# The fourth product of C and B in an accumulator bank, and the low inputs last in the first group of the mixer's output product

## The chip, the core and the metric

The kernel runs on one core of a Trainium2 chip. The metric is device time in microseconds (us) of one execution of the whole program. The core has a tensor engine (TensorE; PE for its matmuls and PEld for its weight loads in the profile), a vector engine (VectorE, DVE), an activation engine (ScalarE, ACT), a general engine (GpSimd, POOL) and a queue engine that issues transfers (SyncE, SP). Matmuls write into PSUM, which this kernel uses as eight banks of 128 x 512 floats.

## What is computed

The reference is a decoder trunk of two layers over 256 tokens of width 1024. Each layer has a SwiGLU feed-forward half step, a mixer, and a second feed-forward half step. The mixer is cut here to the parts that the change touches.

```python
def ssd_chunked(x, dt, a, Bm, Cm):                      # Mamba-2, chunks of 128 tokens
    ...
    cb = jnp.einsum("bclgn,bcsgn->bclsg", Cc, Bc)       # 4 groups g, 2 chunks c
    y_diag = jnp.einsum("bclsg,bclsgh,bcsghp->bclghp", cb, decay, xdt)
    ...
for l in range(DEPTH):
    h = h + 0.5 * swiglu(rms_norm(h, ffn1_norm[l]), ffn1_w_in[l], ffn1_w_out[l])
    u = rms_norm(h, mix_norm[l])
    (z_s, xbc, dt_s, qkv, z_d, b_d, a_d, gate_s, gate_d) = jnp.split(u @ w_in[l], split_points, axis=-1)
    y_s = mamba2_branch(z_s, xbc, dt_s, ...)
    y_d = deltanet_branch(qkv, z_d, b_d, a_d, ...)
    merged = (jax.nn.sigmoid(gate_s) * (y_s @ ssm_w_branch[l])
              + jax.nn.sigmoid(gate_d) * (y_d @ dn_w_branch[l]))
    h = h + merged @ w_out[l]
    h = h + 0.5 * swiglu(rms_norm(h, ffn2_norm[l]), ffn2_w_in[l], ffn2_w_out[l])
return rms_norm(h, final_norm)
```

## The kernel before

**Split products.** Every large product is made from a high and a low half of each factor: `hi` is the value rounded to a shorter format, `lo` what the rounding left. `mm3` (line 334) issues three matmuls for each block: high input times high weight (line 335), high input times low weight (line 336), low input times high weight (line 337). Below they are called A, B and C. `mm3w` and `tok_chunk` (lines 339 to 374) do the same with the roles of weight and input turned.

**Weights.** They stream from memory as tiles of 128 x 1024, issued by SyncE at line 171 into five buffers (`wraw`). `prep` (line 174) makes `whi` on ScalarE (the helper of line 68) and `wlo` on VectorE (the helper of line 71), each in five buffers. `take` (line 202) hands the next weight tile to the product that uses it and prepares up to five ahead.

**Order.** The kernel is written as one sequence. A planner puts it in order for each engine when the program is built, by the sequence, by priorities (work inside `tc.high_priority` comes 400 places earlier) and by its own estimate of when each instruction's inputs and buffers are ready. On the chip each engine then runs its list in that order and waits where an input is not ready. In the mixer the sequence follows a list of names, `ORDER` (line 46): the last part that matters here reads `x01 R d3 R R P R g100 g101 D0 S0 x10 T0 D1 x11 g110 g111 S1 x20 T1`. `R` advances the DeltaNet recurrence (`recur`), `P` is `ssd_pre`, `g` a gate product (`tok_chunk`, tile `t`), `D` the decay matrices (`decay`, tile `dc`, on VectorE and ScalarE), `x` a convolved product (tile `xs`, then three VectorE steps `ca` and a ScalarE step into `xsT`), `S` the head of one Mamba group (`ssd`: eight transposes `xsb` of `xsT`, then VectorE products), `T` its tail.

**PSUM.** Eight banks lie in two pools of four: `accb` (tag "acc") for accumulated products, `trb` (tag "tr") for transposes and short products. A tile of a pool can be written when an earlier tile's last reader is done.

**The product of C and B.** `ssd_pre` makes it for four groups (line 1043). For each group two matmuls (lines 1045 and 1046) write a bank `cbb`, VectorE masks two of its blocks into `cbm`, and ScalarE copies the third into `cbx` (both are parts of the tile `cbt`). All four banks come from the "tr" pool. Just ahead of it in the sequence the recurrence's last chunk takes "tr" banks too; the last of them is `ob` (line 993), which VectorE reads in `vb <- ob, os` (line 998). After that line 1002 to line 1008 square it, reduce it (`so`), take a power on GpSimd, and multiply `vb` by the result.

**The mixer's output product.** The merged branches pass through `merge(t)` (line 1256) for token tile t = 0, then 1: for each half n of the width VectorE makes `mt` and `tg`, TensorE transposes it (`mT`, line 1264), ScalarE makes the high input `mh` and VectorE the low input `ml`. Both calls run at high priority. Then `close` (line 437) issues `out_chunks` for the eight blocks k of the inner width: k = 0 and 1 as one group, k = 2 alone, and k = 3 to 7 as one group. A group goes through token tile 0 and then token tile 1. For tile 0 the order is n = 0 with all k, then n = 1 with all k, and each (k, n) issues A, B and C. The inputs of k = 0 to 3 all come from the transposed half n = 0 of `merge`. Each output bank `o` is an "acc" bank: `po[t][n]`. `close` is called nowhere else.

Of the kernel before, what the change touches and what calls it, by code (L numbers as in the profile page):

```python
# [24 lines left out]
GS = 4  # L25
# [28 lines left out]
def trunk_kernel(ctx, tc, x, wst, wsm, norms, lpar, rpar, cst, out):  # L54
    nc = tc.nc
    V, A, G, PE = nc.vector, nc.scalar, nc.gpsimd, nc.tensor
# [10 lines left out]
    def act(o, i, func=AF.Copy, **kw):  # L67
        return A.activation(out=o, in_=i, func=func, **kw)  # L68

    def tt(o, a, b, op):  # L70
        return V.tensor_tensor(out=o, in0=a, in1=b, op=op)  # L71
# [15 lines left out]
    def trb(name):  # L87
        return trp.tile([P, 512], F32, tag="tr", name=name)

    def accb(name):  # L90
        return accp.tile([P, 512], F32, tag="acc", name=name)
# [57 lines left out]
    state = {"loaded": 0, "prepped": 0, "taken": 0, "last": None, "hold": False, "behind": {}, "late": {}, "first": 0, "turns": {}, "first_chunk": False, "cap": n_forms}  # L149
# [52 lines left out]
    def take():  # L202
        j = state["taken"]
        state["taken"] = j + 1
        ahead("loaded", limit[min(j + NSPL, n_forms) - 1], load)
        ahead("prepped", min(j + 1 if state["hold"] else j + NSPL, n_forms, state["cap"]), prep)
        return halves.pop(j)
# [126 lines left out]
    def mm3(ps, lh, ll, rh, rl, start, stop):  # L334
        PE.matmul(ps, lh, rh, start=start, stop=False)  # L335
        PE.matmul(ps, lh, rl, start=False, stop=False)  # L336
        return PE.matmul(ps, ll, rh, start=False, stop=stop)  # L337
# [55 lines left out]
                        cut and a == 0 and kt == 1,  # L393
                    )

    def out_chunks(ps, stat, ks, last, group=1, split=False, first=None):

        for g0 in range(0, len(ks), group):
            kk = ks[g0 : g0 + group]
            ws = [(k, take()) for k in kk]  # L400
            for t in range(2):
                order = [(k, n) for n in range(2) for k in range(len(kk))]
                if t == 1 and not split:
                    m = len(kk) - 2 if len(kk) == NSPL else len(kk)
                    order = [(k, n) for k in range(m) for n in range(2)]
                    order += [(k, n) for n in range(2) for k in range(m, len(kk))]
                order = [(k, n, 0, 512) for k, n in order]
                if t == 1 and split:
                    order = [o for o in order if o[1] == 0]
                    order += [(k, 1, c, c + 256) for c in (0, 256) for k in range(len(kk))]  # L410
                state["sums"] = []
                for k, n, c0, c1 in order:
                    k, (wh, wl) = ws[k]
                    sh, sl = stat(k, t)
                    c = slice(n * 512 + c0, n * 512 + c1)
                    begin = k == 0 if first is None else first and t == n == 1
                    bank = ps[t][n][:, c0:c1]
                    if c0:
                        begin, bank = k == kk[0], ps[2][:, 0:256]
                    ins = mm3(bank, sh, sl, wh[:, c], wl[:, c], begin, k == last)  # L420
                    state["sums"].append(ins)

    def residual(po, nw):
        def add(t):
            banks = [(po[t][n][:], n * 512) for n in range(2)]
            if nw is None and t == 1:
                banks.append((po[2][:, 0:256], 768))
            for bank, c0 in banks:
                hv = h[:, t, c0 : c0 + bank.shape[-1]]
                ins = stt(hv, bank, 0.5, hv, ALU.mult, ALU.add)  # L430
            return ins

        if nw is None:
            return add
        norm_in(nw, add)

    def close(po, stat, n_k, nw):

        out_chunks(po, stat, list(range(2)), n_k - 1, group=2)
        out_chunks(po, stat, list(range(2, n_k - NSPL)), n_k - 1)  # L440
        state["hold"] = True
        out_chunks(po, stat, list(range(n_k - NSPL, n_k)), n_k - 1, group=NSPL, split=nw is None)
        return residual(po, nw)
# [149 lines left out]
    def mixer(l, nxt):  # L593
# [444 lines left out]
        def ssd_pre():  # L1038
            BT, CT = late["BC"][:, 0:4], late["BC"][:, 4:8]
            cbt = slots.tile([P, 3 * GS, P], F32, tag="sF", name="cbt")  # L1040
            late["cbx"] = cbx = cbt[:, 2 * GS :]
            late["cbm"] = cbm = cbt[:, : 2 * GS].rearrange("p (g t) l -> p g t l", g=GS)
            for g in range(GS):
                cbb = trb("cbb")
                PE.matmul(cbb[:, 0 : 2 * P], BT[:, g, 0:P], CT[:, g, :], start=True, stop=True)
                PE.matmul(cbb[:, 2 * P : 3 * P], BT[:, g, P : 2 * P], CT[:, g, P : 2 * P], start=True, stop=True)
                tt(
                    cbm[:, g],
                    cbb[:].rearrange("p (t o l) -> p t o l", t=2, o=2)[:, :, 0, :],
                    U[:, None, :].to_broadcast([P, 2, P]),  # L1050
                    ALU.mult,
                )
                act(cbx[:, g], cbb[:, P : 2 * P])
            yield
# [123 lines left out]
        def branch(kind, n, mk, tail=1):  # L1178
            ps = [[accb("b"), accb("b")] for _ in range(2)]
            held = {}  # L1180

            def stat(k, t):
                oh, ol = held[k // 2]
                return oh[:, k % 2, t * P : (t + 1) * P], ol[:, k % 2, t * P : (t + 1) * P]

            made = 1
            for j0 in list(range(n - tail)) + [n - tail]:
                js = range(j0, j0 + (tail if j0 == n - tail else 1))
                while made < min(js[-1] + 2, n):
                    mk(made)  # L1190
                    made += 1
                for j in js:
                    held[j] = brT.pop((kind, j))
                out_chunks(ps, stat, [2 * j + i for j in js for i in range(2)], 2 * n - 1, group=2 * len(js))
            return ps
# [13 lines left out]
        def step(name):  # L1209
# [10 lines left out]
            elif kind == "M":  # L1220
                masks()
            elif kind == "I":
                next(inv, None)
            elif kind == "R":
                next(rc, None)
            elif kind == "b":
                bcm(*num)
            elif kind == "d":
                zdm(*num)
            elif kind == "x":  # L1230
                xs_unit(*num)
            elif kind == "P":
                drain(ssd_pre())
            elif kind == "D":
                decay(*num)
            elif kind == "g":
                gate(*num)
            elif kind == "S":
                heads[num[0]] = ssd(*num)
                next(heads[num[0]])  # L1240
            elif kind == "T":
                drain(heads[num[0]])
            elif kind == "o":
                dn_T(0)
            elif kind == "y":
                ss_T(0)
            elif kind == "N":
                dn_branch()
# [4 lines left out]
        ps = branch("s", 8, ss_T)  # L1253
# [20 lines left out]
        po = [[accb("o"), accb("o")] for _ in range(2)]  # L1274

        def stat(k, t):
            return mh[:, k, t * P : (t + 1) * P], ml[:, k, t * P : (t + 1) * P]

        close(po, stat, 8, nxt)

    norm_first(nw0)
# [157 lines left out]
```

## Time and profile before

| what | us |
|---|---|
| median of three runs (lowest, highest) | 1544.98 (1544.69, 1545.77) |
| the profiled execution, its own time | 1543.84 |
| span from its first to its last instruction | 1542.1 |
| VectorE, ScalarE, GpSimd busy in the span | 1229.8, 949.8, 82.6 |
| granted TensorE clock, mean | 0.999 |

How to read it: all stretches below are times from the start of the span. A timeline row has the start, the duration, the engine, the line of the kernel, the operation, output tile and input tiles, the shape and the count of merged instructions; in square brackets stands how long the engine was idle before it, and what ended that idle time. A matmul's end is modelled, so for TensorE the starts are read, and the idle time of the weight loads (PEld). Much of VectorE's and ScalarE's work carries line 71 or 68, the lines of small helpers, so the tile names tell which step it is. The mixer of layer 0 lies at about 400 us to 600 us, that of layer 1 at about 1160 us to 1360 us.

### The profile page before, as it was taken

To read this page: it belongs to the slowest core of one execution; us is meant where nothing else is said; L and a number is where in the kernel's file an instruction comes from. 1 tells how busy PE (TensorE), PEld (TensorE's weight loads), DVE (VectorE), ACT (ScalarE), POOL (GpSimd) and SP (SyncE) were. 2 spreads that over 40 slices of the span, in tenths; PEclk is the share of its full clock that TensorE was granted. 3 is DMA by queue.
4 is the path that set the end of the run, shared out by engine and by line. 5 is a ranking of instruction groups with operands and counts; after the bars stand their busy time and mean duration, and the time that the engine had idled before them with its cause. 6 is when DMAs were issued, how large, how long until landed. Compare 5 with 4: busy or idle time off the path is not lost.

```text
span 1542.1 us, 29082 instructions
## 1 busy us (share of the span) xinstructions
PE 1525.1 (99%) x11473; PEld 1385.3 (90%) x11473; DVE 1229.8 (80%) x1859; ACT 949.8 (62%) x1536; POOL 82.6 (5%) x92
## 2 busy tenths in 40 slices
PE   8999999999999999999999999999999999999998
PEld 7999879999988888999899998899998888899997
DVE  5878768967899766789778887689579996678886
ACT  5656667766665645566555566776756666455565
POOL 0000010000000000000100012010000000000010
PEclk9999999999999999999999999999999999999999
DMA  7687765553565556577866687566346555556775
GB/s 272 187 266 227 232 223 174 183 164 112 180 209 172 157 174 191 184 252 217 264 221 227 204 254 238 182 196 186 117 137 204 180 167 187 175 179 191 250 241 156
DMA packets 98831, 305.73 MB, mean 198 GB/s; under 512 B 22837, under 2 KB 23813, under 8 KB 97670
## 3 DMA queue, kind: packets, MB, share of 16 engines
q1 hardware_dynamic: 93796, 290.95, 57.1%
q0 software_dynamic: 4608, 12.58, 5.0%
q8 instruction: 90, 1.47, 0.4%
q14 instruction: 47, 0.39, 0.1%
q10 hardware_dynamic: 290, 0.33, 0.1%
HBM read 297.72 MB, written 1.92 MB: 194 GB/s over the span
## 4 chain that ended last, share of the span: by engine, by line
PE 90%; DVE 3%; ACT 3%; DMA 2%; issue 1%; POOL 0%; SPq 0%; POOLq 0%; ACTq 0%; DVEq 0%
PE fc L346 10%; PE fc L340 9%; PE fc L345 9%; PE t L366 9%; PE o L337 4%; PE o L336 4%; PE o L335 4%; PE f L366 3%; PE b L337 3%; PE b L335 3%; PE b L336 3%; PE p L336 2%; PE p L335 2%; PE p L337 2%; PE xs L340 1%; PE xs L345 1%
## 5 line engine op out<-in xcount | busy, mean ns | idle before, releaser
L71 DVE TENSOR_TENSOR wlo<-wraw,whi 128x1024 fp32r<-128x1024 f32 x488 | 592.2, 1222 | 189.9 <-ACT whi L68 175.4
L68 ACT ACTIVATE whi<-wraw 128x1024 fp32r<-128x1024 f32 x488 | 511.4, 1059 | 266.8 <-PE fc L345 87.3
L346 PE MATMUL fc<-uW,wlo 128*128 128x256 f32 x1280 | 354.9, 277 | 0.0
L340 PE MATMUL fc<-uW,whi 128*128 128x256 f32 x1280 | 354.1, 277 | 0.0
L345 PE MATMUL fc<-uW,whi 128*128 128x256 f32 x1260 | 348.3, 276 | 0.0
L340 PEld LDWEIGHTS fc<-uW,whi 128*128 128x128 f32 x1280 | 240.5, 188 | 0.8
L346 PEld LDWEIGHTS fc<-uW,wlo 128*128 128x128 f32 x1280 | 240.5, 188 | 0.0
L345 PEld LDWEIGHTS fc<-uW,whi 128*128 128x128 f32 x1260 | 236.5, 188 | 0.8
L366 PE MATMUL t<-whi,uW 128*128 128x512 f32 x512 | 165.4, 397 | 0.0
L366 PEld LDWEIGHTS t<-whi,uW 128*128 128x128 f32 x512 | 95.9, 188 | 21.6 <-issue 1.3
L68 ACT ACTIVATE whi<-wsum 128x1024 fp32r<-128x1024 f32 x64 | 68.0, 1062 | 58.7 <-PE fc L345 32.3
L366 PE MATMUL t<-wlo,uW 128*128 128x512 f32 x256 | 100.1, 392 | 0.0
L71 DVE TENSOR_TENSOR wlo<-wsum,whi 128x1024 fp32r<-128x1024 f32 x64 | 78.2, 1222 | 8.3 <-ACT whi L68 5.9
L335 PE MATMUL b<-whi,bh 128*128 128x512 f32 x192 | 76.1, 398 | 0.3 <-ACT bh L68 0.2
L336 PE MATMUL b<-wlo,bh 128*128 128x512 f32 x192 | 75.0, 390 | 0.0
L337 PE MATMUL b<-whi,bl 128*128 128x512 f32 x192 | 74.3, 394 | 0.3 <-DVE bl L71 0.3
L340 PE MATMUL xs<-uW,whi 128*128 128x256 f32 x256 | 72.8, 284 | 0.0
L346 PE MATMUL xs<-uW,wlo 128*128 128x256 f32 x256 | 71.4, 279 | 0.0
L345 PE MATMUL xs<-uW,whi 128*128 128x256 f32 x254 | 70.5, 278 | 0.0
L335 PE MATMUL o<-whi,gh 128*128 128x512 f32 (+1 forms) x160 | 62.0, 388 | 0.0
L337 PE MATMUL o<-whi,gl 128*128 128x512 f32 (+1 forms) x160 | 61.8, 386 | 0.0
L336 PE MATMUL o<-wlo,gh 128*128 128x512 f32 (+1 forms) x160 | 61.7, 386 | 0.0
(337 smaller groups left out, 3301.2 us busy)
## 6 DMA issues: line engine op xcount, KB each, us to landing
wraw<-in_wst_dram SPq DMA_DIRECT2D x504, 512.0 KB, 4.8
wsum<-in_wst_dram SPq DMA_DIRECT2D x16, 512.0 KB, 7.3
wsum<-in_wst_dram POOLq DMA_DIRECT2D x16, 512.0 KB, 8.6
dc<-rdram SPq DMA_DIRECT2D x8, 1024.0 KB, 8.6
nw<-in_norms_dram SPq DMA_DIRECT2D x6, 512.0 KB, 5.3
h<-u POOLq DMA_DIRECT2D x12, 256.0 KB, 6.4
gb<-rdram SPq DMA_DIRECT2D x8, 256.0 KB, 6.1
h<-in_x_dram SPq DMA_DIRECT2D x4, 256.0 KB, 3.7
```

The lines of the kernel that those rows point to most:

```text
L68: return A.activation(out=o, in_=i, func=func, **kw)
L71: return V.tensor_tensor(out=o, in0=a, in1=b, op=op)
L335: PE.matmul(ps, lh, rh, start=start, stop=False)
L336: PE.matmul(ps, lh, rl, start=False, stop=False)
L337: return PE.matmul(ps, ll, rh, start=False, stop=stop)
L340: PE.matmul(ps, wh, mh, start=start, stop=False)
L345: PE.matmul(ps, wh, ml, start=False, stop=False)
L346: PE.matmul(ps, wl, mh, start=False, stop=stop)
L366: ins = PE.matmul(ps[t][:], st, mv, start=k0 == 0 and j == 0, stop=k0 == KT - 2 and j == 5)
```

## The change

There are two edits. In `ssd_pre` the fourth group's `cbb` (g = 3) is taken from the "acc" pool; the other three stay in the "tr" pool. In `out_chunks` a new argument `defer` changes the order within token tile 0: A and B are issued for every (n, k) of the group, and the C products follow behind them all, in the same order of (n, k). `close` sets it for its first group (k = 0 and 1) alone. No instruction is added or removed.

```diff
-    def out_chunks(ps, stat, ks, last, group=1, split=False, first=None):
+    def out_chunks(ps, stat, ks, last, group=1, split=False, first=None, defer=False):
...
-                state["sums"] = []
+                state["sums"], lows = [], []
                 for k, n, c0, c1 in order:
...
                         begin, bank = k == kk[0], ps[2][:, 0:256]
+                    if defer and t == 0:
+                        PE.matmul(bank, sh, wh[:, c], start=begin, stop=False)
+                        PE.matmul(bank, sh, wl[:, c], start=False, stop=False)
+                        lows.append((bank, sl, wh[:, c]))
+                        continue
                     ins = mm3(bank, sh, sl, wh[:, c], wl[:, c], begin, k == last)
                     state["sums"].append(ins)
+                for bank, sl, high in lows:
+                    PE.matmul(bank, sl, high, start=False, stop=False)
...
     def close(po, stat, n_k, nw):
 
-        out_chunks(po, stat, list(range(2)), n_k - 1, group=2)
+        out_chunks(po, stat, list(range(2)), n_k - 1, group=2, defer=True)
...
             for g in range(GS):
-                cbb = trb("cbb")
+                cbb = trb("cbb") if g < GS - 1 else accb("cbb")
```

## The prediction

> **What bounds the kernel now.** I read the page first, then the waits of the weight loads, then the timeline around the two places of the change.
>
> ```profile
> span 1542.1 us, 29082 instructions
> PE 1525.1 (99%) x11473; PEld 1385.3 (90%) x11473; DVE 1229.8 (80%) x1859; ACT 949.8 (62%) x1536; POOL 82.6 (5%) x92
> PE 90%; DVE 3%; ACT 3%; DMA 2%; issue 1%; POOL 0%; SPq 0%; POOLq 0%; ACTq 0%; DVEq 0%
> ```
>
> TensorE is busy for 1525.1 of 1542.1 us, and 90% of the chain that ended last is TensorE. So time can be won only where TensorE stands still, and only if the time won is not waited away further on. The waits of the weight loads say where it stands (total us, times, longest):
>
> ```profile
> PEld xsb L1101 <- ACT xsT L68: 2.1, 2, 1.1
> PEld cbb L1045 <- DVE vb L71: 2.0, 2, 1.2
> PEld o L337 <- DVE ml L71: 1.5, 2, 0.7
> ```
>
> The second and third rows are the two waits at which the two edits stand. Together they are 3.5 us, the most that both edits can give. The first row belongs to neither edit, but it comes about 40 us behind the second in the same mixer.
>
> **Part 1, the fourth product of C and B.** Layer 0, with the wait of layer 1 at the end:
>
> ```profile
> 403.38 2.29 DVE L71 TENSOR_TENSOR dc<-dc,ac 128x2048 f32<-128x2048 f32 x1 [0.64 <-DMA dc<-rdram]
> ...
> 405.36 0.19 PEld L366 LDWEIGHTS t<-whi,uW 128*128 128x128 f32 x1
> 405.59 0.68 DVE L71 TENSOR_TENSOR vb<-ob,os 128x512 f32<-128x512 f32 x1
> 406.33 0.30 PEld L1045 LDWEIGHTS cbb<-BC 128*128 128x128 f32 x2 [0.77 <-DVE vb L71]
> 406.97 0.69 DVE L1004 TENSOR_REDUCE so<-o 128x4 f32<-128x512 f32 x1
> 407.98 0.42 DVE L71 TENSOR_TENSOR cbt<-cbb,cs 128x256 f32<-128x256 f32 x1
> 409.18 0.69 DVE L71 TENSOR_TENSOR vb<-vb,so 128x512 f32<-128x512 f32 x1 [0.78 <-POOL so L210]
> ...
> 1168.62 0.30 PEld L1045 LDWEIGHTS cbb<-BC 128*128 128x128 f32 x2 [1.20 <-DVE vb L71]
> ```
>
> The fourth `cbb` waits for the bank that `ob` holds. VectorE reads `ob` only behind the 2.29 us subtraction of the decays, which itself waited for a transfer. In an accumulator bank this wait goes if such a bank is free. The last two holders are done:
>
> ```profile
> 397.68 1.52 DVE L74 SCALAR_TENSOR_TENSOR ca<-xs,lp,ca 128x255 f32<-128x255 f32 x3 [0.48 <-ACT ca L68]
> 401.39 0.58 ACT L68 ACTIVATE zdT<-zd 128x512 f32<-128x512 f32 x1
> ```
>
> The `xs` bank was last read at 399.20 and the `zd` bank at 401.97. The gate's two banks `t` are the other two, so two of four are free at 405.36. TensorE therefore arrives earlier by 0.77 us in layer 0 and by 1.20 us in layer 1, 1.97 together. No instruction is added, no transfer moves, and the mask and copy of the fourth group keep their places.
>
> But is TensorE then the one that is waited for? VectorE from 409.18 on, in both layers:
>
> ```profile
> core 0: us, PE busy (x) PEld busy (x) DVE busy (x) ACT busy (x) POOL busy (x), PEclk, DMA share, GB/s
> 409.20:445.50 36.30, 35.90 (x273) 31.61 (x271) 35.70 (x43) 25.70 (x33) 1.60 (x1) 1.00 0.53 174
> 1171.50:1207.80 36.30, 36.11 (x273) 31.81 (x271) 35.70 (x43) 25.70 (x33) 1.60 (x1) 1.00 0.55 173
> ```
>
> VectorE is busy for 35.70 of 36.30 us. Its only pause in the stretch of layer 0, and what stands at the end of each stretch:
>
> ```profile
> 436.69 1.23 DVE L71 TENSOR_TENSOR wlo<-wraw,whi 128x1024 fp32r<-128x1024 f32 x1 [0.60 <-ACT whi L68]
> ...
> 445.00 0.48 DVE L74 SCALAR_TENSOR_TENSOR ca<-xs,lp,ca 128x253 f32<-128x253 f32 x1
> 445.57 0.42 ACT L68 ACTIVATE xsT<-ca 128x256 f32<-128x256 f32 x1 [1.26 <-DVE ca L74]
> 446.03 0.20 PEld L1101 LDWEIGHTS xsb<-cs,xsT 128*128 128x128 f32 x2 [1.13 <-ACT xsT L68]
> ...
> 1208.34 0.20 PEld L1101 LDWEIGHTS xsb<-cs,xsT 128*128 128x128 f32 x2 [0.93 <-ACT xsT L68]
> ```
>
> The pause waits for ScalarE, not for TensorE. So the train of VectorE work that begins at 409.18 ends at 445.48 whatever TensorE does between. Its own start hangs on the reduction at 406.97 and GpSimd, which hang on `vb` at 405.59 and the transfer before 403.38; none of these is touched. The two last `xsb` transposes wait for the end of that train. TensorE comes 0.77 us earlier and waits 1.13 + 0.77 = 1.90 us there; in layer 1 it waits 0.93 + 1.20 = 2.13 us. **Part 1 comes to 0.** From the other sides: -1.97 us if nothing takes the time back, for which the planner would have to put the two transposes later among the `xs` products; +0.42 us a layer, 0.84 in all, if the fourth group's mask (0.42 us at 407.98) is now planned ahead of the reduction and pushes the whole train. I take 0, because TensorE ran other work (the row at 405.36) just once before the fourth product and then stood, though more of that work was ready behind it. The planner thus expected the bank after one such matmul, saw no wait, and has no reason to place `xsb` anew.
>
> [...]
>
> **Part 2, the low inputs last.** Layer 0 (layer 1 has the same wait: 1.5 us in two times, by the third row of the waits above):
>
> ```profile
> 572.50 0.19 PEld L335 LDWEIGHTS o<-whi,mh 128*128 128x128 f32 x1
> ...
> 573.19 0.19 PEld L336 LDWEIGHTS o<-wlo,mh 128*128 128x128 f32 x1
> 573.39 0.68 DVE L71 TENSOR_TENSOR ml<-mT,mh 128x512 fp32r<-128x512 f32 x1
> 573.99 0.68 DVE L71 TENSOR_TENSOR tg<-tg,mt 128x512 f32<-128x512 f32 x1
> 574.12 0.19 PEld L337 LDWEIGHTS o<-whi,ml 128*128 128x128 f32 x1 [0.74 <-DVE ml L71]
> 574.78 0.50 PEld L1264 LDWEIGHTS mT<-cs,tg 128*128 128x128 f32 x4
> 575.56 0.60 ACT L68 ACTIVATE mh<-mT 128x512 fp32r<-128x512 f32 x1 [1.53 <-PE mT L1264]
> 576.30 0.19 PEld L335 LDWEIGHTS o<-whi,mh 128*128 128x128 f32 x1
> 576.99 1.21 DVE L71 TENSOR_TENSOR wlo<-wraw,whi 128x1024 fp32r<-128x1024 f32 x1
> ```
>
> The loads at 572.50 and 573.19 are the first and the fourth, so one matmul takes (573.19 - 572.50) / 3 = 0.23 us. After four of them (A and B of two blocks in different banks) everything left needs C first, and C needs `ml`, done at 573.39 + 0.68 = 574.07. With the change eight A and B are free to run. The eighth loads at 572.50 + 7 x 0.23 = 574.11, and the C products behind it find `ml` done. The wait of 0.74 us goes, in both layers 1.48.
>
> Now what is late next: token tile 1. Its first product needs `mh` of that tile, and that hangs on VectorE again: `tg` ends at 574.67, the transposes `mT` load at 574.78, `mh` runs from 575.56 to 576.16, and the first product of tile 1 loads at 576.30. I count twelve matmuls of tile 0 before it, seven ahead of `mT` and five behind. Nothing in `tg`, `mT` and `mh` gets earlier, because VectorE's list (with two weight halves `wlo` of over 1.2 us in it) is untouched. If TensorE does not stand, (574.78 - 572.50) / 0.23 = 9.9, so ten matmuls are done when `mT` can go; `mT` takes 0.50, the last two end at 574.78 + 0.50 + 0.46 = 575.74, and TensorE stands until 576.16. So the first product of tile 1 comes earlier by 576.30 - 576.16 = 0.14 us, and not by 0.74. **Part 2 comes to 2 x 0.14 = 0.28 us.** Bounds: 0, if the planner leaves `mT` behind seven matmuls, so that TensorE stands before `mT` instead; -1.48, if it fills the gap with tile 0 of k = 2, whose inputs (same half n = 0) are ready. I take 0.28 since `mh` bounds it for any order that keeps tile 1 next in the sequence. Behind this place no later wait of the weight loads is pinned to VectorE until the next mixer, so what is won here stays.
>
> **The sum.** Within the profiled span of 1542.1 us: 0 - 0.28 = -0.3 us. The profiled execution took 1543.84 us, 1.74 more than its span and 1.14 less than the median of the runs; neither offset is touched, so I apply the difference to the median: 1544.98 - 0.3 = **1544.7 us**.
>
> **Rivals.**
> *All of it is kept.* 1.97 + 1.48 = 3.45 us, 1541.5 us. For it: TensorE is the bound of the kernel as a whole, and both waits are real idle time of the weight loads. Against it: the two windows of VectorE and the rows at 575.56 and 576.30. It needs the planner to place `xsb` later and to fill before tile 1. [...]
> *Only one part is kept whole.* 1.97 or 1.48 us, so 1543.0 or 1543.5 us.
> *A weight half gets ahead of a pinned train (the other side).* The order on VectorE is planned anew from other estimates, and in each of the two dense stretches a `wlo` of about 1.22 us is put ahead of what TensorE waits for: ahead of `tg` near 573.99, and ahead of the last `ca` before 445. It decides once `tg` ends more than 0.14 us later; from there TensorE loses one for one. Price per layer 1.21 - 0.14 = 1.07, plus 1.23 at `xsb`: 2.30, over two layers 4.6 us, 1549.6 us. For it: VectorE has no slack in either stretch, and such a `wlo` stands right behind the train (576.99). Against it: `merge` runs at high priority, and no VectorE instruction changes.
> *The change does not do what it says.* The planner already moved A and B of another bank ahead of C by itself; it could undo the written order. Then 1545.0 us.
>
> **How the numbers follow.** Forecast 0.38, all kept 0.24, one part kept 0.05, slower by a weight half 0.30, no effect 0.03. A measurement of this kernel tells 0.2%, about 3.1 us, from no change. The forecast, one part and no effect lie within it: 0.46. All kept, 3.45 us or 0.22%, lies just over it: faster 0.24. The weight half lies over it: slower 0.30. The forecast's own range runs from -1.97 - 1.48 x 0.5 to +0.84, so 1542.3 to 1545.8. The range for 8 in 10 takes in both rivals: 1541.4 to 1549.7.
>
> **What would show it.** The rows `cbb <- DVE vb` gone and `xsb <- ACT xsT` grown from 2.1 to about 4.0 us would show part 1 right; `xsb` still near 2.1 would show it wrong. In part 2 `o L337 <- DVE ml` should be gone, and a wait of about 0.4 us on `mh` before the first `o L335` of tile 1, or one on `tg` before `mT`, should stand in its place. A VectorE train in another order at 409 to 445 or 572 to 579, with `xsb` or `mT` later than now, would make the forecast wrong on the slow side; products of k = 2 ahead of tile 1 on the fast side.

## The result, and the profile after

The changed kernel takes 1547.16 us (median of 14 runs, 1544.37 to 1550.55), beside 1544.80 us for the kernel before in the same comparison (14 runs, 1542.81 to 1547.27). The ratio is 1.0019, with a 95% interval of 1.0011 to 1.0026: about 3 us slower by the ratio and 2.4 us by the medians, where 0.3 us faster was forecast. That is above the forecast's own range (1542.3 to 1545.8); it lies inside the range for 8 in 10 only because that one took in the rival on the slow side. The difference is inside the bound of 0.2%, but its interval excludes no change, on the other side. From line 422 of the old numbering on, every line of the changed kernel stands 7 lines further down.

The page of the kernel after, span and busy times, and its chain of waits:

```profile
span 1545.4 us, 29084 instructions
PE 1526.4 (99%) x11473; PEld 1386.5 (90%) x11473; DVE 1229.4 (80%) x1859; ACT 949.1 (61%) x1536; POOL 84.8 (5%) x92
PE 85%; DVE 7%; ACT 2%; DMA 2%; issue 1%; POOL 1%; SPq 1%; POOLq 0%; ACTq 0%; DVEq 0%
```

The span grew by 3.3 us. TensorE's busy time grew by 1.3 us and GpSimd's by 2.2 us though neither got an instruction more (the two more in the total are in no engine's count), and VectorE's share of the chain went from 3% to 7%. The waits of the weight loads after (total, times, longest):

```profile
PEld xsb L1108 <- ACT xsT L68: 5.0, 2, 2.6
...
PEld pst L671 <- ACT smT L68: 2.2, 2, 2.0
...
PEld b L335 <- ACT bh L68: 1.8, 5, 0.6
...
PEld b L337 <- DVE bl L71: 1.5, 2, 0.7
```

The two rows of before that the edits aimed at, `cbb <- DVE vb` (2.0 us) and `o <- DVE ml` (1.5 us), are gone from the head of the list. `xsb` went from 2.1 to 5.0 us. (`pst` stands 200 us ahead of the changed code, and its wait differs from execution to execution: 0.9 us in the trace before, 2.3 us in a second trace of the changed kernel.)

The start of the fourth group's work in layer 0 after the change, and the two GpSimd rows of layer 1:

```profile
401.77 0.30 PEld L1052 LDWEIGHTS cbb<-BC 128*128 128x128 f32 x2
...
403.31 0.42 DVE L71 TENSOR_TENSOR cbt<-cbb,cs 128x256 f32<-128x256 f32 x1
...
404.42 2.29 DVE L71 TENSOR_TENSOR dc<-dc,ac 128x2048 f32<-128x2048 f32 x1 [0.70 <-DMA dc<-rdram]
...
408.01 0.69 DVE L1011 TENSOR_REDUCE so<-o 128x4 f32<-128x512 f32 x1
...
409.02 1.22 DVE L78 TENSOR_SCALAR dc<-dc 128x2048 f32<-128x2048 f32 x1
...
409.18 1.92 POOL L210 TENSOR_TENSOR so<-so,mhalf 128x4 f32<-128x4 f32 x1 [18.45 <-DVE so L74]
...
411.14 0.69 DVE L71 TENSOR_TENSOR vb<-vb,so 128x512 f32<-128x512 f32 x1 [0.90 <-POOL so L210]
...
1172.81 1.92 POOL L210 TENSOR_TENSOR so<-so,mhalf 128x4 f32<-128x4 f32 x1 [18.69 <-DVE so L74]
```

The order is new. A `cbb` is made and masked ahead of `ob` now (401.77 and 403.31), so one mask stands ahead of the subtraction, and no mask is left to fill the time while GpSimd takes its power. The planner put the next ready piece there: the clamp of the decays (409.02, line 78), which before stood behind `vb <- vb, so`. Beside the clamp GpSimd's power takes 1.92 us and not 1.01 (before: 408.13 and 1170.44), so `vb <- vb, so` comes 411.14 - 404.42 = 6.72 us behind the start of the subtraction, where before it was 409.18 - 403.38 = 5.80.

The `xsb` wait of layer 0 after, and the weight loads behind it:

```profile
447.38 0.20 PEld L1108 LDWEIGHTS xsb<-cs,xsT 128*128 128x128 f32 x2 [2.41 <-ACT xsT L68]
...
447.89 0.26 PEld L340 LDWEIGHTS xs<-uW,whi 128*128 128x128 f32 x1
448.04 0.34 PEld L345 LDWEIGHTS xs<-uW,whi 128*128 128x128 f32 x1
448.26 0.33 PEld L346 LDWEIGHTS xs<-uW,wlo 128*128 128x128 f32 x1
...
451.24 0.25 PEld L345 LDWEIGHTS xs<-uW,whi 128*128 128x128 f32 x1
451.43 0.19 PEld L346 LDWEIGHTS xs<-uW,wlo 128*128 128x128 f32 x1
...
1211.00 0.20 PEld L1108 LDWEIGHTS xsb<-cs,xsT 128*128 128x128 f32 x2 [2.57 <-ACT xsT L68]
```

The same stretch, and the one behind it, as windows (TensorE clock third from the end):

```profile
447.30:451.30 4.00, 3.92 (x21) 3.92 (x22) 3.64 (x6) 0.03 (x1) 0.00 (x0) 0.58 0.74 231
451.30:455.30 4.00, 4.00 (x81) 3.81 (x81) 2.46 (x3) 3.24 (x4) 0.00 (x0) 0.99 0.17 44
```

Here is a cost that no term of the forecast held. Half a microsecond behind the wait the loads go from 0.19 to 0.33 us each, one every 0.21 us in place of 0.11, and they stay so from about 447.95 to 451.3. In four microseconds 21 matmuls start; in the same stretch behind the wait of before it is 35. TensorE counts as busy all the while, which fits the growth of its busy time. About 3.35 us at half clock would cost half of that, an estimated 1.7 us, unless a later wait takes some of it back. The longer wait of layer 1 (1211.00) has no such stretch behind it in this trace.

The kernel before, the four microseconds behind its own `xsb` waits of 1.13 and 0.93 us:

```profile
446.00:450.00 4.00, 3.96 (x35) 3.97 (x36) 4.00 (x7) 1.06 (x1) 0.00 (x0) 1.00 0.83 248
1208.30:1212.30 4.00, 3.96 (x34) 3.96 (x35) 4.00 (x7) 1.01 (x1) 0.00 (x0) 1.00 0.83 235
```

And the output product in layer 0 after, with its first and its last load:

```profile
576.19 0.19 PEld L421 LDWEIGHTS o<-whi,mh 128*128 128x128 f32 x1
...
577.80 0.19 PEld L422 LDWEIGHTS o<-wlo,mh 128*128 128x128 f32 x1
578.03 0.19 PEld L428 LDWEIGHTS o<-whi,ml 128*128 128x128 f32 x1
578.48 0.42 PEld L1271 LDWEIGHTS mT<-cs,tg 128*128 128x128 f32 x4 [0.27 <-issue]
578.87 0.53 PEld L428 LDWEIGHTS o<-whi,ml 128*128 128x128 f32 x3
...
579.17 0.60 ACT L68 ACTIVATE mh<-mT 128x512 fp32r<-128x512 f32 x1 [1.44 <-PE mT L1271]
579.43 0.19 PEld L335 LDWEIGHTS o<-whi,mh 128*128 128x128 f32 x1
...
579.83 0.19 PEld L335 LDWEIGHTS o<-whi,mh 128*128 128x128 f32 x1 [0.20 <-ACT mh L68]
...
580.55 0.19 PEld L337 LDWEIGHTS o<-whi,ml 128*128 128x128 f32 x1 [0.19 <-DVE ml L71]
...
599.76 0.19 PEld L337 LDWEIGHTS o<-whi,ml 128*128 128x128 f32 x1
```

Lines 421, 422 and 428 are the A, B and C of the edit. Eight A and B run, then a C that no longer waits, as written. From the first load to the last it takes 599.76 - 576.19 = 23.57 us. The last load of the same product in the kernel before:

```profile
596.49 0.19 PEld L337 LDWEIGHTS o<-whi,ml 128*128 128x128 f32 x1
```

That is 596.49 - 572.50 = 23.99 us, so this edit does win 0.42 us in layer 0. That points to the other edit for the loss.

### The profile page after: what moved, and what is told of

Same layout as the page of the kernel before. It is cut to its first block, busy times and chain, and to the rows that moved or that the text cites. A ratio compares the mean times of both kernels' runs of the same rounds, so it can differ in the third digit from the quotient of the medians.

```text
span 1545.4 us, 29084 instructions
## 1 busy us (share of the span) xinstructions
PE 1526.4 (99%) x11473; PEld 1386.5 (90%) x11473; DVE 1229.4 (80%) x1859; ACT 949.1 (61%) x1536; POOL 84.8 (5%) x92
## 3 DMA queue, kind: packets, MB, share of 16 engines
HBM read 297.72 MB, written 1.92 MB: 194 GB/s over the span
## 4 chain that ended last, share of the span: by engine, by line
PE 85%; DVE 7%; ACT 2%; DMA 2%; issue 1%; POOL 1%; SPq 1%; POOLq 0%; ACTq 0%; DVEq 0%
PE fc L346 9%; PE fc L340 9%; PE fc L345 9%; PE t L366 7%; PE o L337 4%; PE o L336 4%; PE o L335 4%; PE f L366 3%; PE b L337 3%; PE b L336 3%; PE b L335 3%; DVE wlo L71 2%; PE p L336 2%; PE p L337 2%; PE p L335 2%
```

## The experiments

Each was timed beside the kernel before on the same chip. The "mean clock" is the mean over the timed runs of the TensorE clock that the core was granted. In the thirteen traces 0.999 goes with no spell of half clock in a mixer, 0.998 with one and 0.997 with two; the rest is the end of the span, which ran at half clock with no matmul left to do (the last 4.3 us in the trace of before, the last 1.8 us in the trace after). The kernel before had medians of 1544.80, 1545.29, 1544.86 and 1544.31 us in the four sets of comparisons, so rows of different sets are compared by their ratios, which are not quotients of the medians.

| kernel | median us | ratio to before, interval | mean clock |
|---|---|---|---|
| before (beside the two edits alone, product held, clamp behind) | 1545.29 | | 0.9989 |
| changed | 1547.16 | 1.0019 (1.0011 to 1.0026) | 0.9980 |
| changed, once more | 1547.47 | 1.0012 (1.0002 to 1.0022) | 0.9980 |
| bank alone | 1549.88 | 1.0026 (1.0016 to 1.0036) | 0.9973 |
| low inputs last alone | 1544.49 | 0.9990 (0.9981 to 1.0000) | 0.9989 |
| bank, its product held | 1556.74 | 1.0072 (1.0059 to 1.0086) | 0.9952 |
| bank, clamp behind | 1549.97 | 1.0030 (1.0018 to 1.0042) | 0.9972 |
| bank, mask behind (old order) | 1545.82 | 1.0010 (1.0001 to 1.0019) | 0.9983 |
| both edits, mask behind | 1544.90 | 1.0004 (0.9994 to 1.0013) | 0.9981 |
| the last, `xsb` later | 1554.61 | 1.0063 (1.0050 to 1.0076) | 0.9952 |
| before, convolutions ahead | 1546.72 | 1.0008 (0.9999 to 1.0016) | 0.9988 |
| low inputs last, convolutions ahead | 1545.41 | 1.0005 (0.9997 to 1.0014) | 0.9988 |
| changed, convolutions ahead | 1548.59 | 1.0020 (1.0011 to 1.0029) | 0.9978 |

**Each edit alone.**

```diff
-                cbb = trb("cbb")
+                cbb = trb("cbb") if g < GS - 1 else accb("cbb")
```

> The bank of the fourth product alone. Theory 1 (the bank let the planner rearrange the start of VectorE's train, the clamp of the decays now runs beside GpSimd's power of so, the train comes about 0.9 us later in each layer, and TensorE pays that and sometimes a lower granted clock at the last xsb): 2 to 4 us slower than before, so a ratio of about 1.0013 to 1.0026; the cbb wait is gone, xsb waits of about 2.4 and 2.6 us, GpSimd's so at about 1.9 us. Theory 2 (the bank is worth its 1.97 us or nothing, and the loss of the whole change comes from the low inputs last): within 0.5 us of before, or up to 2 us faster.

The bank alone costs 0.26%, some 4 us. Its start in layer 0 and 1 is that of the changed kernel, with GpSimd at 1.92 us in both. Theory 1 holds for the order and the size of the loss. The `xsb` waits in its trace were shorter than it named, 1.95 and 1.74 us, with no half clock behind them; the traced execution was the fastest of the twelve.

The other one is the edit of `out_chunks` and `close` alone.

> The low inputs last alone. Theory 1: the wait on ml gone, about 0.4 us a layer won, so 0.8 us faster than before (ratio about 0.9995); mixer unchanged with cbb waits of 0.77 and 1.20 and xsb waits near 1.1 and 0.9. The prediction's own sum for this part: 0.28 us faster. Theory 2: 2 us or more slower, since the loss of the whole change would then be here.

0.10% faster, about 1.5 us by the ratio and 0.8 us by the medians, with an interval that reaches no change. In its trace the product takes 23.53 us from first to last load in both layers, against 23.99 and 24.00 us before, so 0.46 us a layer. Within their intervals the two edits alone add up (1.0026 and 0.9990 against 1.0019), so nothing here shows that they disturb each other. Theory 2 falls.

**Which part of the new order costs.** First the fourth product's matmuls were held behind those of the third:

```diff
+                with ExitStack() as behind:
+                    if g == GS - 1:
+                        behind.enter_context(tc.issue_after(third.ins))
                     PE.matmul(cbb[:, 0 : 2 * P], BT[:, g, 0:P], CT[:, g, :], start=True, stop=True)
```

> The bank of the fourth product, with the two matmuls of that product kept behind those of the third in the planner's order, so that vb stands ahead of the clamp on VectorE as before. Theory 1: GpSimd's so back to about 1.0 us, xsb waits no longer than the prediction's 1.9 and 2.1 us, and the time within 1 us of before. Theory 2 (the loss has nothing to do with the order at the start of VectorE's train): as slow as the bank alone.

GpSimd's power was back at 1.01 us and the `xsb` waits at 0.5 us, but the kernel was 0.7% slower. The planner had arranged the whole stretch anew: in each layer the first `b` product now waits 3.6 us for `bh`, with half clock behind it. As a test of the cause it tells nothing, since more moved than was meant; it shows how far one held product reaches.

Then the clamp itself was held behind `vb <- vb, so`:

```diff
-            ts(dv, dv, 0.0, ALU.min)
+            with tc.issue_after(late["normed"].ins):
+                ts(dv, dv, 0.0, ALU.min)
```

> The bank of the fourth product, with the clamp of the decays issued behind the product of vb and so. Theory 1: GpSimd's so back from 1.9 to about 1.0 us and vb about 0.9 us earlier against its reduction; the time 1 to 3 us less than the bank alone. Rival (GpSimd's power takes 1.9 us for a reason that has nothing to do with the clamp beside it): so stays at about 1.9 us.

Both missed. The planner filled the place with the next piece, the 2.29 us subtraction of the second group. The rows of layer 0:

```profile
409.35 2.29 DVE L71 TENSOR_TENSOR dc<-dc,ac 128x2048 f32<-128x2048 f32 x1
...
409.51 2.99 POOL L210 TENSOR_TENSOR so<-so,mhalf 128x4 f32<-128x4 f32 x1 [18.59 <-DVE so L74]
412.54 0.69 DVE L71 TENSOR_TENSOR vb<-vb,so 128x512 f32<-128x512 f32 x1 [0.90 <-POOL so L210]
```

GpSimd now takes 2.99 us. It ends 0.86 us behind the subtraction (409.51 + 2.99 against 409.35 + 2.29), and in the changed kernel it ends 0.86 us behind the clamp (409.18 + 1.92 against 409.02 + 1.22). So in both kernels it ends only when the large VectorE operation is done, whichever that is. Why it does so, no run shows.

**The old order with the new bank.** What keeps VectorE's order is the mask in the gap. So the fourth group's mask was held behind the scaling of `so`:

```diff
+                with ExitStack() as behind:
+                    if g == GS - 1:
+                        behind.enter_context(tc.issue_after(late["scaled"].ins))
                     tt(
                         cbm[:, g],
```

Now VectorE, ScalarE, GpSimd and the queues have the order of the kernel before, instruction by instruction, and on TensorE only the fourth product moved ahead. This is the very case that the forecast summed.

> The bank of the fourth product, with that group's mask held behind the scaling of so, so that VectorE, ScalarE, GpSimd and the queues have exactly the order of the kernel before and only TensorE's fourth product stands earlier. This is the condition under which the prediction summed part 1 to 0. Theory 1 (the loss comes from VectorE's new order alone): the cbb wait gone, GpSimd's so at 1.0 us, xsb waits of about 1.9 and 2.1 us, no half clock, the time within 0.5 us of before. Theory 2 (the loss comes from the length of the xsb wait, by the half clock behind it): the same waits, but a mean clock of about 0.998 over the runs and 1 to 2 us slower than before. Rival (the bank is worth what it removes): 2 us faster.

The start, the two `xsb` waits, the first load of the output product in each layer, and the windows behind the waits:

```profile
404.08 2.29 DVE L71 TENSOR_TENSOR dc<-dc,ac 128x2048 f32<-128x2048 f32 x1 [1.02 <-DMA dc<-rdram]
...
408.84 1.01 POOL L210 TENSOR_TENSOR so<-so,mhalf 128x4 f32<-128x4 f32 x1 [18.51 <-DVE so L74]
409.88 0.69 DVE L71 TENSOR_TENSOR vb<-vb,so 128x512 f32<-128x512 f32 x1 [0.79 <-POOL so L210]
...
446.73 0.29 PEld L1104 LDWEIGHTS xsb<-cs,xsT 128*128 128x128 f32 x2 [2.22 <-ACT xsT L68]
...
574.34 0.19 PEld L335 LDWEIGHTS o<-whi,mh 128*128 128x128 f32 x1
...
1166.17 2.29 DVE L71 TENSOR_TENSOR dc<-dc,ac 128x2048 f32<-128x2048 f32 x1 [0.81 <-DMA dc<-rdram]
...
1208.82 0.20 PEld L1104 LDWEIGHTS xsb<-cs,xsT 128*128 128x128 f32 x2 [2.01 <-ACT xsT L68]
...
1335.30 0.19 PEld L335 LDWEIGHTS o<-whi,mh 128*128 128x128 f32 x1
```

```profile
446.70:450.70 4.00, 3.96 (x21) 3.97 (x22) 4.00 (x7) 0.00 (x0) 0.00 (x0) 0.58 0.76 245
1208.80:1212.80 4.00, 3.98 (x35) 3.98 (x36) 4.00 (x7) 1.06 (x1) 0.00 (x0) 1.00 0.83 249
```

The `xsb` waits are 2.22 and 2.01 us; the forecast had 1.90 and 2.13. In layer 0 the transposes come at the same distance from the start of the subtraction as before: 446.73 - 404.08 = 42.65 us, against 446.03 - 403.38 = 42.65. So the train is pinned as the forecast said, and TensorE's earlier arrival is waited away whole. But the kernel is still 0.10% slower (1.5 us, with an interval that only just excludes no change), and this trace shows where: in layer 0 the wait is followed by half clock (21 matmuls, clock 0.58), in layer 1 it is not (35 matmuls, 1.00). From the subtraction to the first load of the output product layer 0 takes 574.34 - 404.08 = 170.26 us and layer 1 takes 1335.30 - 1166.17 = 169.13; in the four layers of the kernel before and of the low inputs alone it is 168.7 to 169.1 us. Its four runs at a clock of 0.999 took 1545.12 us on average, the four at 0.998 took 1546.51, and the two at 0.997 and 0.996 took 1548.51 and 1549.71. The kernel before ran at 0.999 in 16 of its 21 runs there, at 1544.28 on average, so some 0.8 us of the difference is not tied to the clock by these rounded figures. Theory 2 holds in the main: a longer wait in the same place costs time although nothing on VectorE is late.

> The same with the low inputs last as well: the whole change under the old order of VectorE in the mixer. Theory 1: 0.8 us faster than before, like the low inputs alone, and 2 to 3 us faster than the changed kernel. Theory 2: about as slow as the changed kernel, or 1 us better.

0.04% above before, interval on both sides of 1: the low inputs pay back about what the half clock takes. That is 1 to 2 us better than the changed kernel (1.0019 and, timed once more, 1.0012), about as theory 2 said, but the intervals overlap; and it is not better than before.

**The changed kernel a second time.**

> The changed kernel once more, for a second trace of the same order. Theory 1: the order on each engine and the xsb waits of about 2.4 us are the same, and what differs in time goes with the granted clock: each stretch of half clock behind an xsb wait is about 3.4 us long and costs about 1.7 us. Theory 2 (the spread of the changed kernel comes from transfers that land earlier or later): the time differs with the waits on transfers and the clock is the same in both traces.

The waits and what lies behind them:

```profile
447.68 0.20 PEld L1108 LDWEIGHTS xsb<-cs,xsT 128*128 128x128 f32 x2 [2.16 <-ACT xsT L68]
...
1210.84 0.20 PEld L1108 LDWEIGHTS xsb<-cs,xsT 128*128 128x128 f32 x2 [2.20 <-ACT xsT L68]
```

```profile
447.60:451.60 4.00, 3.92 (x33) 3.92 (x34) 3.65 (x6) 1.09 (x2) 0.00 (x0) 1.00 0.85 236
1210.80:1214.80 4.00, 3.96 (x23) 3.96 (x24) 3.61 (x6) 0.00 (x0) 0.00 (x0) 0.64 0.78 239
```

This time the half clock is in layer 1. In the first trace it was in layer 0, though the longer wait (2.57 us) stood in layer 1. So the event belongs to the execution, not to the place, and which layers are hit is what spreads the times. Theory 1 holds in kind; the transfers differ too (the wait of a layer's first subtraction for `dc` ranges from 0.25 to 2.10 us over the traces), so the spread isn't the clock's alone.

**Filling or moving the wait.** Three kernels plan the convolutions of one `xs` unit at high priority, so that their `ca` steps stand ahead of weight halves:

```diff
+            with ExitStack() as ahead_:
+                if (g, i) == (1, 1):
+                    ahead_.enter_context(tc.high_priority(offset=PRI))
                 for a in range(2):
                     conv(
```

> The kernel before with the same convolutions at high priority, neither edit made. Theory 1: the xsb waits of 1.1 and 0.9 us gone, 1 to 2 us faster than before. Theory 2 (wlo late instead): no difference, with new waits of TensorE on wlo in place of the ones at xsb.

> The low inputs last without the bank, and the same convolutions at high priority. Theory 1: the xsb waits of 1.1 and 0.9 us gone, the 0.8 us of the low inputs kept, so 2 to 2.8 us faster than before, about 1542.5, clock 0.999. Theory 2 (the weight halves that are moved behind the ca products are late for TensorE, a wait on wlo takes the place of the one at xsb): within 0.8 us of the low inputs alone.

> Both edits of the change, and the convolutions of the second unit of the second group planned at high priority, so that the ca products which the last xsb transposes wait for stand ahead of weight halves wlo on VectorE; nothing else of the changed kernel's order moves. Theory 1 (the loss of the change is the long wait at xsb with the half clock behind it in some executions, plus about 1 us a layer at the b products): xsb waits well below 2.4 us, no half clock at that place, mean granted clock back at 0.999, 2 to 4 us less than the changed kernel, so 1543 to 1545.5 and at or below before. Theory 2 (the loss lies at the b products and later, whatever happens at xsb): still 1 to 3 us slower than before.

The numbers of theory 2 about held (for the second by the medians, 0.9 us apart; by the ratios it is 2.3 us), its reason in none: TensorE waited for no `wlo` in that stretch. Without the bank the `xsb` wait is gone and the clock stays at 0.9988, but no time is won. The waits of the kernel before with that edit:

```profile
PEld b L335 <- ACT bh L68: 3.5, 4, 1.0
PEld cbb L1045 <- DVE vb L71: 3.4, 2, 2.2
```

The wait on `bh` at the `b` products went from 1.0 to 3.5 us, presumably because steps that were passed are late now. (The 2.2 us at `cbb` goes with a late transfer: the subtraction ahead of it waited 2.10 us for `dc`.) With the bank the planner also moved the two transposes seven matmuls ahead, so the waits stayed at 2.8 and 2.4 us, the half clock came in layer 0, and nothing was won.

The last one planned the transposes later among the `xs` products, at a lower priority (`offset=-40` for k = 3 of that group):

> The same as the whole change under the old order, but the last two xsb transposes planned about 12 matmuls later among the products of xs; the order behind them changes from there on. Theory 1 (VectorE is the bound from the start of the decays to the b products, so a wait filled at one place comes back at the next): xsb waits of about 0.5 us, longer waits on bh and bl at the b products, and no gain over the low inputs alone. Rival (the wait at xsb is real and can be filled): 2 to 4 us faster than before.

`xsb` waits 0.6 and 1.1 us, but `yT` 2.0 and `b` 3.6 us in each layer, and the half clock there lasts twice as long. In layer 0 it begins 0.6 us before the wait on `bh` ends, in layer 1 0.8 us behind the wait of `yT`:

```profile
466.27 0.28 PEld L335 LDWEIGHTS b<-whi,bh 128*128 128x128 f32 x1 [3.61 <-ACT bh L68]
```

```profile
466.20:472.20 6.00, 5.93 (x14) 4.67 (x15) 5.95 (x9) 1.41 (x4) 0.00 (x0) 0.50 0.37 117
```

Theory 1 was right on where the wait would come back, and far off in the price. Of all these kernels only the low inputs alone come out below before, with an interval that reaches 1.0000.

## Why the prediction failed, point by point

**What bounds the stretch: right.** VectorE's train from the start of the decays sets when `xsb` can go. With VectorE's order kept the distance from subtraction to `xsb` is the same to 0.02 us in both layers, and the waits are 2.22 and 2.01 us where 1.90 and 2.13 were forecast.

**"The mask and copy of the fourth group keep their places": wrong, and the first failed step.** It was drawn from TensorE's wait alone. That the planner "has no reason to place `xsb` anew" all but held: the two transposes stand one `xs` product later. But with the bank free the planner put the product ahead of `ob`; the masks shifted by one; and the gap in which VectorE waits for GpSimd, which the fourth mask had filled, was given to the clamp. So the start of the train, of which "none of these is touched" was said, was touched. The rival on the slow side named this kind of event, a replanned VectorE with a large piece ahead of what is waited for, but with a `wlo` at another place and 2.30 us a layer. The price of the new order can be read from the traces: `xsb` comes 447.38 - 404.42 = 42.96 us behind the subtraction, against 42.65. That is 0.31 us in layer 0, and 0.28 us in layer 1. It is less than the 0.92 us by which `vb` is late, because the train behind `vb` got shorter. The forecast's bound of 0.42 us a layer for a train that is pushed held as far as `xsb`, with another cause. Behind `xsb`, where the order on VectorE and TensorE is new too, more is lost. Layer 1 of the trace after, without half clock:

```profile
1168.05 2.29 DVE L71 TENSOR_TENSOR dc<-dc,ac 128x2048 f32<-128x2048 f32 x1 [0.86 <-DMA dc<-rdram]
...
1338.10 0.19 PEld L421 LDWEIGHTS o<-whi,mh 128*128 128x128 f32 x1
```

From the subtraction to the output product that is 170.05 us. In the four layers with this order and no half clock (changed kernel twice, bank alone) it is 169.8 to 170.2 us; in six with the old order and no half clock (before, low inputs alone, the two kernels with the mask behind) 168.7 to 169.5. So the new order costs about 1 us a layer by itself.

**A wait was priced as its own length: the second failed step.** The sum moved 0.77 and 1.20 us from one wait to another and called that 0. It is 0 for VectorE's train. But two waits of about 1 us each had become one of 2 us and more, and behind such a wait TensorE ran at half clock for about 3.4 us in some executions. The layers of the last paragraph's kernels that had it took 0.6 to 1.7 us longer to the output product than the other layer of the same trace. With the old order kept it is the only loss that the trace shows, in a kernel that is 0.10% slower; without it, in layer 1 there, the sum of 0 came out about as forecast. None of the four traces without the bank has such a spell in a mixer, eight of the nine with it have one or more. No term, bound or rival of the forecast held it. From the old order to the new one (1.0010 to 1.0026) is another 2.5 us, about, though the two were not timed side by side and their intervals overlap. About 2 us is the new order's 1 us a layer; the mean clock falls by 0.0010 between the two, which is an estimated 1.5 us (0.0010 x 1545). Together that is more than the 2.5, within what the two intervals leave open. This split is read from traces, and no run was made to test it. The waits on `bh` and `bl` at the `b` products are no sure part of it: 1.7 us before, 3.3 us in the trace after, 1.9 us in the second trace of the same kernel.

**Part 2: the mechanism right, the size off.** The wait of 0.74 us on `ml` is gone, and a wait of 0.20 us on `mh`, where about 0.4 was named, and one of 0.19 us on `ml` of tile 1 stand in its place. The gain is 0.42 to 0.46 us a layer in place of 0.14. The term that was mis-sized is the count of twelve products ahead of the `mh` of tile 1: thirteen are loaded before that wait (eight A and B, four C, and the one at 579.43). The first that waits loads 579.83 - 576.19 = 3.64 us into the stage, against 576.30 - 572.50 = 3.80 before, so 0.16 us earlier where 0.14 was forecast; the thirteenth product is the other 0.23. Its kind isn't named in the trace. By the written sequence it should be tile 0 of k = 2, the case that the bound of -1.48 had allowed for. VectorE's list was not "untouched" here either: the `tg` of the next `mT` now stands behind an `ml`, and the `mh` that hangs on it starts 6.37 us behind the first load (582.56) and not 5.12 (577.62). The product still ends earlier.

**What would show it.** `cbb <- DVE vb` gone and `xsb` grown to 5.0 us where 4.0 was named: by these two rows alone part 1 would have passed as right. The sign for the slow side, a VectorE train in another order at 409 to 445 with `xsb` later than now, is the one that came. What the list lacked was the clock behind the wait.

**The rival "all of it is kept": right on the gap, wrong on the gain.** The bank does remove the wait at `cbb` (0.77 and 1.20 us before) in every kernel that has it. As a gain it fails even with all else kept (1.0010), since TensorE, which had the gap, is not the bound of that stretch: VectorE is, busy for 35.70 of 36.30 us before.

## What to carry to other kernels

A freed buffer is a change of the plan, not of one wait: compare the order of every engine before costing it, and look first at the gaps that the moved pieces used to fill. Where another engine pins the stretch, removing a wait only gathers it at the next place (here `xsb` went from 1.13 and 0.93 us to 2.22 and 2.01), and a gathered wait can cost more than its parts: here waits of 2 us and more were sometimes followed by a spell of half clock, those of 1.2 us or less never. Where the pinned engine cannot be made faster, two short waits may be the better choice.

## What the runs showed of the hardware that was not expected

**Half clock around waits of 2.0 to 3.6 us.** In the mixers it came behind single waits of 2.02, 2.20, 2.22, 2.41 and 2.77 us at `xsb` and of 2.81 and 2.86 us at the `b` products, and lasted about 3.4 us (a clock of 0.58 over 4.00 us, as in two of the traces, is 0.42 x 4.00 / 0.50 = 3.4 us of half clock). It did not come behind others of 1.95, 2.01, 2.16, 2.42 and 2.57 us at `xsb` and of 2.23 us at `cbb`. Around a wait of 3.61 us it came in all four cases, once for about 3.4 us and three times for about 6.8, in two of these with a wait of 2.0 us at `yT` just ahead. It came behind no wait below 2.0 us. What decides in a given execution is open: a wait of 1.99 us at `pst` in the trace after had full clock behind it, and no run varied the wait's length alone.

**A small GpSimd operation that ends only behind a large one of VectorE.** The power of 128 x 4 numbers took 1.01 us in the old order, beside the 0.42 us mask, 1.92 us beside the 1.22 us clamp, and 2.99 us beside the 2.29 us subtraction, in the last two cases ending 0.86 us behind the VectorE operation. What ties the two together was not shown.
